# A hybrid attention layer on one core: the first attention's values and probabilities as scaled fp16 halves, two heads' values on chip, and the second attention's buffers laid out anew

## The chip, the cores and the metric

The kernel runs on one core of one Trainium2 chip. The metric is the device time of one execution in microseconds; the kernel before takes 2904.12 us (median of 3 runs, 2902.68 to 2909.47). PE is the matrix engine, with its weight loads shown apart as PEld; DVE, ACT and POOL are the vector, scalar and general engines; SP issues the DMAs.

## The reference, cut to what matters

One layer on a sequence of 1024 positions with 1024 channels: a feed-forward block, two attentions side by side on one normalised input, a gated merge of both, a second feed-forward block. The change touches the two attentions, above all the first:

```python
def diff_attention(q, k, v, cos, sin, lam_params, head_gain, lam_init):
    # q, k: 8 heads x 2 maps x 64;  v: 8 heads x 128;  T = 1024, causal
    q = apply_rope(q, cos, sin)
    k = apply_rope(k, cos, sin)
    lam = exp(sum(lp[0] * lp[1])) - exp(sum(lp[2] * lp[3])) + lam_init
    def block(i):                                  # 128 queries
        s = einsum('bqhcd,bkhcd->bhcqk', qb, k) * scale
        p = softmax(where(kpos <= qpos, s, NEG_INF))
        a = p[:, :, 0] - lam * p[:, :, 1]          # difference of the two maps
        return einsum('bhqk,bkhe->bqhe', a, v)
    o = rmsnorm(o, head_gain) * (1.0 - lam_init)
```

The second attention (16 heads of 64, two groups that share keys and values) adds a compressed, a selected and a window branch, each with its own softmax. With 16 blocks of which 16 are selected, the selected branch is causal attention over all blocks.

## The kernel before

**Precision.** Products that need more than one pass are made of two parts: a value is split into a high part (`hi`, a copy by ACT to a shorter type) and a rest (`lo`, a subtraction by DVE). `split` (L89, L85) makes fp32r parts; `split16` and the second attention make fp16 parts. `mm3` (L52 to L54) adds the three products hi·hi, hi·lo and lo·hi. Transposes, scores and projections work on 4-byte operands.

**Order of the work.** A first feed-forward block; `prelim`, which projects keys, values and queries for the second attention, its compressed branch, and the first two heads' values of the first attention; `da_phase`, the first attention; `ns_phase`, the second attention; `proj`, the merge; a second feed-forward block. The instructions are emitted in program order with priorities; a planner puts each engine's queue in order by priority and by its own model of time. `K.tc.high_priority(offset=-n)` sets a stretch of code n places back. Tiles come from pools opened on a stack; a pool that closes gives its space to later ones, and a tile on that space waits for the last use of the tile that lay there.

**Values of the first attention.** `v_da_unit(K, h)` projects the values of a head in two halves of 512 positions (`tb`). The product goes to a bank `gm`, is scaled by DVE to `vt` (L650), transposed by four matmuls (L653) into another tile of `gm`, split by ACT and DVE into `vh` and `vl`, and both are stored to DRAM (`s_v`, L658). `da_load_parts` loads a head's keys (L1031) and both parts of its values (L1038) at the start of the head; the pool of values holds one head (two tiles).

**The first attention.** `da_phase` goes through eight heads in four steps `m` of 256 queries. `da_queries` loads queries; `da_scores` makes two maps of scores in a pair of banks (L909), finds the maximum with DVE (L916), exponentiates with ACT into tiles `Pt` (L918), and combines the maps with POOL and DVE (L948 to L952). One step later `finish` calls `da_pv`: `tr_split` transposes up to four blocks into a bank `tr` (L964) and splits them to `th` and `tl`; three matmuls for each pair of blocks add to `o` (L991 to L993). After every second step `da_finish` copies `o` to `ob`, and one step later `da_finish2` normalises it with a chain over PE (L1008), ACT, POOL and DVE (L1014) and stores `yo` (L1018).

**The filler.** Between scores, `Filler` emits parts of independent products at a low priority: the units of `da_units` for heads 4 to 7 (queries, keys, values), then 16 gate units and 8 of the projection `pda_unit`, which reads the stored result of the first attention. `fill.pace(units, steps)` spreads them over the steps. In the filler there is one `gm` bank.

**The second attention.** `ns_phase` opens its pools on the space of the first attention's, loads queries, values and masks, and goes through 16 heads with the same scheme: `ns_scores` writes probabilities to a tile `P0` and a window tile `P1` from a ring of six pairs (two in one pool, four in another), `ns_pv` adds to `o` with fp16 operands (L1146, L1147).

Of the kernel before, what the change touches and what calls it, by code (L numbers as in the profile page):

```python
# [7 lines left out]
F32 = mybir.dt.float32  # L8
# [10 lines left out]
P = 128  # L19
# [623 lines left out]
def v_da_unit(K, h):  # L643
    nc = K.nc
    w = load_w(K, K.A["win"][C_VDA + h])
    for tb in range(NTB):
        ps = K.gm.tile([P, TB], F32, tag="gm", name="gm")
        yield from fill_gemm(K, ps, w, K.h[tb])
        vt = K.mp.tile([P, TB], F32, tag="m13", name="vt")
        nc.vector.tensor_tensor(out=vt, in0=ps, in1=K.R[tb], op=ALU.mult)  # L650
        tr = K.gm.tile([P, 4, P], F32, tag="gm", name="tr")
        for j in range(4):
            nc.tensor.transpose(tr[:, j], vt[:, j * P:(j + 1) * P], K.ident)  # L653
        vh = K.mp.tile([P, 4, P], F32R, tag="rh", name="vh")
        vl = K.mp.tile([P, 4, P], F32R, tag="rl", name="vl")
        split(nc, vh, vl, tr)
        for hl, t in ((0, vh), (1, vl)):
            nc.sync.dma_start(out=K.s_v[h][hl][:, tb * 4:tb * 4 + 4], in_=t.bitcast(F32))  # L658
# [300 lines left out]
def tr_split(K, blocks):  # L959
# [5 lines left out]
    dt = F16 if K.narrow else F32R  # L965
    hi = K.tp.tile([P, TB], dt, tag="th", name="th")
    lo = K.tp.tile([P, TB], dt, tag="tl", name="tl")
    if K.narrow:
        nc.scalar.activation(out=hi[:, 0:n], in_=tr[:, 0:n], func=AF.Copy)  # L969
        nc.vector.tensor_tensor(out=lo[:, 0:n], in0=tr[:, 0:n], in1=hi[:, 0:n], op=ALU.subtract)  # L970
    else:
        split(nc, hi[:, 0:n], lo[:, 0:n], tr[:, 0:n])
# [48 lines left out]
def da_load(K, h):  # L1021
    drain([da_load_parts(K, h)])


def da_load_parts(K, h):
    nc = K.nc
    p, s0 = h // 2, (h % 2) * 2
    K.k = []
    for c in range(2):
        t = K.kp.tile([P, T], F32R, tag="k", name="kt")  # L1030
        nc.sync.dma_start(out=t.bitcast(F32), in_=K.s_k[p][:, :, s0 + c].rearrange("h a d t -> (h a) d t"))  # L1031
        K.k.append(t)
        yield
    K.v = []
    K.vv[h] = K.v
    for hl in range(2):
        t = K.vp.tile([P, 8, P], F32R, tag="v", name="vt")
        nc.sync.dma_start(out=t.bitcast(F32), in_=K.s_v[h][hl])  # L1038
        K.v.append(t)
        yield  # L1040
# [676 lines left out]
```

## Time and profile before

| what | value |
|---|---|
| median of 3 runs | 2904.12 us (2902.68 to 2909.47) |
| the profiled execution | 2903.55 us, span 2901.8 us |
| mean granted clock of PE | 0.988 |
| PE busy | 2791.5 us, 96% of the span |
| DVE, ACT, POOL busy | 1995.2, 1370.8, 789.2 us |
| DMA | 476.12 MB, mean 164 GB/s |

The span runs from the first to the last instruction. PE's busy time counts overlapping matmuls once, and the ends of matmuls are modelled, so the rate of PE is better read from one start to the next. The first attention lies at about 975 to 1472 us, the second at 1472 to 2065. Line numbers are those of the kernel before.

### The profile page before, as it was taken

To read this page: it belongs to the slowest core of one execution; us is meant where nothing else is said; L and a number is where in the kernel's file an instruction comes from. 1 tells how busy PE (TensorE), PEld (TensorE's weight loads), DVE (VectorE), ACT (ScalarE), POOL (GpSimd) and SP (SyncE) were. 2 spreads that over 40 slices of the span, in tenths; PEclk is the share of its full clock that TensorE was granted. 3 is DMA by queue.
4 is the path that set the end of the run, shared out by engine and by line. 5 is a ranking of instruction groups with operands and counts; after the bars stand their busy time and mean duration, and the time that the engine had idled before them with its cause. 6 is when DMAs were issued, how large, how long until landed. Compare 5 with 4: busy or idle time off the path is not lost. (4 is left out here: it accounts for less than half of the span.)

```text
span 2901.8 us, 40199 instructions
## 1 busy us (share of the span) xinstructions
PE 2791.5 (96%) x14278; PEld 2055.0 (71%) x14278; DVE 1995.2 (69%) x3356; ACT 1370.8 (47%) x2351; POOL 789.2 (27%) x701
## 2 busy tenths in 40 slices
PE   8999999999999899989989999999999999999998
PEld 6644447887788778868877778888787844444886
DVE  7866865666688467667777777777333977676566
ACT  7533424442333245445566666677433653333443
POOL 3134321000045212322233333333242414223001
PEclk9999999999999999999999999999999999999999
DMA  4355547655446645444432226222843246445854
GB/s 164 121 202 179 177 170 269 217 189 148 153 174 211 221 155 177 167 162 160 155 122 89 88 80 201 88 88 81 315 149 120 80 146 221 163 171 172 293 182 144
DMA packets 212137, 476.12 MB, mean 164 GB/s; under 512 B 20832, under 2 KB 39520, under 8 KB 211936
## 3 DMA queue, kind: packets, MB, share of 16 engines
q1 hardware_dynamic: 211936, 473.55, 48.1%
q8 instruction: 112, 1.84, 0.3%
q14 instruction: 89, 0.73, 0.1%
HBM read 312.52 MB, written 160.96 MB: 163 GB/s over the span
## 5 line engine op out<-in xcount | busy, mean ns | idle before, releaser
L405 PEld LDWEIGHTS <-w 128*128 128x128 f16 x3024 | 297.3, 99 | 381.8 <-issue 32.2
L52 PE MATMUL gm<-hi,whi 128*128 128x512 f32 x880 | 351.0, 399 | 6.0 <-ACT whi L89 3.3
L54 PE MATMUL gm<-hi,wlo 128*128 128x512 f32 x880 | 348.7, 397 | 0.5 <-DVE wlo L85 0.5
L53 PE MATMUL gm<-lo,whi 128*128 128x512 f32 x880 | 348.0, 395 | 0.0
L405 PE MATMUL Y<-tf,w 128*128 128x512 f16 x1296 | 297.5, 384 | 16.7 <-DVE u L443 13.9
L909 PE MATMUL S<-kt,qt 128*128 128x320 f32 (+5 forms) x1152 | 270.1, 352 | 27.2 <-ACT Pt L918 12.4
L85 DVE TENSOR_TENSOR wlo<-st,whi 128x1024 fp32r<-128x1024 f32 x154 | 197.6, 1301 | 114.2 <-ACT whi L89 113.2
L916 DVE CUSTOM_DVE_ANT_0 S<-S,slab 128x896 f32<-128x896 f32 (+7 forms) x320 | 224.3, 710 | 56.1 <-PE S L909 50.3
L53 PE MATMUL acc<-wlo,whi 128*128 128x512 f32 (+1 forms) x628 | 244.4, 389 | 1.0 <-DVE wlo L85 1.0
L89 ACT ACTIVATE whi<-st 128x1024 fp32r<-128x1024 f32 x154 | 160.7, 1057 | 178.8 <-PE acc L54 106.4
L54 PE MATMUL acc<-whi,wlo 128*128 128x512 f32 (+1 forms) x628 | 243.0, 390 | 0.0
L52 PE MATMUL acc<-whi 128*128 128x512 f32 (+1 forms) x628 | 240.7, 387 | 0.4 <-DVE xd L590 0.4
L970 DVE TENSOR_TENSOR tl<-tr,th 128x512 f16<-128x512 f32 (+2 forms) x304 | 183.9, 616 | 45.9 <-ACT th L969 44.9
L909 PEld LDWEIGHTS S<-kt,qt 128*128 128x128 f32 x1152 | 182.7, 190 | 43.9 <-ACT Pt L918 14.6
L1098 POOL TENSOR_SCALAR Ps<-Ps,l 128x384 f32<-128x384 f32 (+7 forms) x128 | 102.0, 797 | 372.6 <-DVE l L1096 246.0
L969 ACT ACTIVATE th<-tr 128x512 f16<-128x512 f32 (+2 forms) x304 | 159.2, 539 | 79.0 <-PE tr L964 62.6
L405 PE MATMUL X<-h,w 128*128 128x512 f16 x864 | 195.3, 379 | 0.6 <-ACT s L415 0.5
L52 PEld LDWEIGHTS gm<-hi,whi 128*128 128x128 f32 x880 | 168.1, 191 | 39.0 <-ACT whi L89 3.5
L54 PEld LDWEIGHTS gm<-hi,wlo 128*128 128x128 f32 x880 | 167.8, 191 | 36.3 <-DVE wlo L85 1.4
L53 PEld LDWEIGHTS gm<-lo,whi 128*128 128x128 f32 x880 | 167.7, 191 | 30.8
L85 DVE TENSOR_TENSOR wlo<-wst,whi 128x1024 fp32r<-128x1024 f32 x103 | 137.9, 1340 | 45.6 <-ACT whi L89 36.8
L521 POOL TENSOR_TENSOR u<-u,u 128x512 f32<-128x512 f32 x36 | 52.8, 1467 | 345.0 <-DVE sa L102 163.2
(330 smaller groups left out, 6167.9 us busy)
## 6 DMA issues: line engine op xcount, KB each, us to landing
wst<-in_win_dram SPq DMA_DIRECT2D x55, 512.0 KB
sw<-w2s SPq DMA_DIRECT2D x44, 512.0 KB
st<-sw SPq DMA_DIRECT2D x88, 256.0 KB
st<-saT SPq DMA_DIRECT2D x88, 256.0 KB
a<-in_f1w_dram SPq DMA_DIRECT2D x36, 512.0 KB
a<-in_f2w_dram SPq DMA_DIRECT2D x36, 512.0 KB
st<-saB SPq DMA_DIRECT2D x66, 256.0 KB
qt<-sq SPq DMA_DIRECT2D x128, 128.0 KB
```

Source lines behind the costliest of these rows:

```text
L52: first = nc.tensor.matmul(out, lhsT=w[0][:, wk], rhs=x[0], start=start, stop=False, skip_group_check=skip)
L53: nc.tensor.matmul(out, lhsT=w[0][:, wk], rhs=x[1], start=False, stop=False, skip_group_check=skip)
L54: nc.tensor.matmul(out, lhsT=w[1][:, wk], rhs=x[0], start=False, stop=stop, skip_group_check=skip)
L85: return nc.vector.tensor_tensor(out=lo, in0=src, in1=hi.bitcast(F32), op=ALU.subtract)
L89: nc.scalar.activation(out=hi, in_=src, func=AF.Copy)
L405: K.mark = nc.tensor.matmul(o, lhsT=w[:, a, m * h + k], rhs=x[k][:, b], start=start and k == 0 and i == 0, stop=k == h - 1 and i == 2, ski ...
L521: nc.gpsimd.tensor_tensor(out=a, in0=a, in1=b, op=ALU.mult)
L909: K.last = nc.tensor.matmul(S[:, o:o + n], lhsT=q, rhs=k[:, k0 + c:k0 + c + n], start=i == 0, stop=i == 1)
L916: nc.vector.tensor_tensor_reduce(out=sv, in0=sv, in1=mv, scale=-0.125, scalar=BIG, op0=ALU.add, op1=ALU.min, accum_out=nm)
L969: nc.scalar.activation(out=hi[:, 0:n], in_=tr[:, 0:n], func=AF.Copy)
L970: nc.vector.tensor_tensor(out=lo[:, 0:n], in0=tr[:, 0:n], in1=hi[:, 0:n], op=ALU.subtract)
L1098: nc.gpsimd.tensor_scalar(out=p[:, 0:n], in0=p[:, 0:n], scalar1=l[:, c:c + 1], scalar2=P_NS, op0=ALU.mult, op1=ALU.mult)
```

## The change

Scores stay as they were. The values are stored once, as fp32; per head, the sum of their squares gives a power of two (`pow2_scale`) by which they are scaled when they are split into fp16 halves on chip. `lam` takes a scale of its own, so that the difference of the maps fits fp16; the inverse of both scales (`dsi`) rides on the copy of `o` to `ob`. The value unit handles two heads and puts the transposes of each half behind the first part of the next product; in the filler they use the `tr` banks instead of `gm`. The value pool holds two heads' halves (four fp16 tiles) and one loaded tile. Values are loaded ahead: at step 2 of the head before (heads 1, 2, 3, 5, 7) or at the start of their own head (4, 6), and split at step 3 of the head before or behind the scores of step 0. `th`/`tl` have three pairs instead of two. The second attention's pools are split up and opened in another order with padding, and the last `da_finish2` gets priority offset -250 instead of -100.

```diff
-def v_da_unit(K, h):
...
+def v_da_unit(K, heads):
+    late = None
+    for h in heads:
+        w = load_w(K, K.A["win"][C_VDA + h])
+        for tb in range(NTB):
+            ps = K.gm.tile([P, TB], F32, tag="gm", name="gm")
+            for k, _ in enumerate(fill_gemm(K, ps, w, K.h[tb])):
+                if k == 0 and late:
+                    v_da_store(K, *late)
+                yield
+            vt = K.mp.tile([P, 2, TB], F32, tag=("m13", "m42")[tb], name="vt")
+            K.nc.vector.tensor_tensor(out=vt[:, 0], in0=ps, in1=K.R[tb], op=ALU.mult)
+            late = h, tb, vt
+    v_da_store(K, *late)
+
+def v_da_store(K, h, tb, vt):
+    nc = K.nc
+    pool, tag = (K.gm, "gm") if K.fill is None else (K.tr, "tr")
+    tr = pool.tile([P, TB], F32, tag=tag, name="tr")
+    for j in range(4):
+        nc.tensor.transpose(tr[:, j * P:(j + 1) * P], vt[:, 0, j * P:(j + 1) * P], K.ident)
+    vr = K.mp.tile([P, 2, TB], F32, tag=("rh", "rl")[tb], name="vr")
+    nc.scalar.activation(out=vr[:, 0], in_=tr, func=AF.Copy)
+    nc.sync.dma_start(out=K.s_v[h][:, tb * 4:tb * 4 + 4], in_=vr[:, 0].rearrange("p (j d) -> p j d", j=4))
+    nc.scalar.activation(out=vt[:, 1], in_=vt[:, 0], func=AF.Square, accum_out=K.dss[:, 2 * h + tb:2 * h + tb + 1])
...
@@ tr_split
-    dt = F16 if K.narrow else F32R
...
+    hi = K.tp.tile([P, TB], F16, tag="th", name="th")
+    lo = K.tp.tile([P, TB], F16, tag="tl", name="tl")
+    nc.scalar.activation(out=hi[:, 0:n], in_=tr[:, 0:n], func=AF.Copy)
+    nc.vector.tensor_tensor(out=lo[:, 0:n], in0=tr[:, 0:n], in1=hi[:, 0:n], op=ALU.subtract)
@@ da_finish
-    nc.scalar.activation(out=ob, in_=o, func=AF.Copy)
+    nc.scalar.activation(out=ob, in_=o, func=AF.Copy, scale=K.dsi[:, h:h + 1])
...
+def da_load_values(K, h):
+    K.vr = K.vrp.tile([P, 8, P], F32, tag="vr", name="vr")
+    K.nc.sync.dma_start(out=K.vr, in_=K.s_v[h])
+
+def da_split_values(K, h, pool, tag):
+    nc = K.nc
+    tot = pool.tile([P, TB], F32, tag=tag, name="tot")[:, 0:1]
+    for tb in range(NTB):
+        nc.tensor.matmul(tot, lhsT=K.ones, rhs=K.dss[:, 2 * h + tb:2 * h + tb + 1], start=tb == 0, stop=tb == 1)
+    s, v = pow2_scale(K, K.cst, tot, 51, K.pinv)
+    nc.vector.tensor_copy(out=K.dsi[:, h:h + 1], in_=v)
+    t = [K.vp.tile([P, 8, P], F16, tag="v", name="vt") for _ in range(2)]
+    nc.scalar.activation(out=t[0], in_=K.vr, func=AF.Copy, scale=s)
+    nc.vector.scalar_tensor_tensor(out=t[1], in0=K.vr, scalar=s, in1=t[0], op0=ALU.mult, op1=ALU.subtract)
+    K.vv[h] = t
...
@@ prelim
+        s, v = pow2_scale(K, K.cst, l2, 51)
+        nc.vector.tensor_scalar(out=K.lam, in0=K.lam, scalar1=s, scalar2=None, op0=ALU.mult)
+        nc.vector.tensor_copy(out=K.pinv, in_=v)
...
-B_DV = 2
+B_DV = 4
...
-B_DT = 2
+B_DT = 3
+PAD = (1152, 1536)
...
@@ da_phase
+                if h in (4, 6):
+                    da_load_values(K, h)
                 for m in range(4):
                     qt = q0 if h + m == 0 else da_queries(K, h, m)
...
+                    if m == 2 and h + 1 in (1, 2, 3, 5, 7):
+                        da_load_values(K, h + 1)
                     res = da_scores(K, h, m, qt, fill.step)
                     if pend:
                         finish(*pend)
+                    if m == 0 and h in (4, 6):
+                        da_split_values(K, h, K.tr, "tr")
+                    if m == 3 and h + 1 in (1, 2, 3, 5, 7):
+                        da_split_values(K, h + 1, K.tr, "tr")
                     pend = (h, m, res)
...
-        with K.tc.high_priority(offset=-100):
+        with K.tc.high_priority(offset=-250):
             da_finish2(K, *K.fin)
...
@@ ns_phase
-        K.pp, K.n_p = [open_pool(K, ctx, "npa", 2), open_pool(K, ctx, "npb", B_NP - 2)], 0
...
+        pad("pad0", PAD[0])
+        K.nvp = {(0, 0): pool("nv00"), (0, 1): pool("nv01")}
+        K.pcp.append(pool("npc1"))
+        K.pp = [None] * B_NP
+        third = pool("pw2")
+        pad("pad1", PAD[1])
+        K.tp = pool("nt", B_NT)
+        K.pp[5] = [pool("ps5")]
+        for i in range(3):
+            K.pp[i] = [pool(f"ps{i}")]
+        K.pp[2].append(third)
+        K.pp[0].append(pool("pw0"))
+        pad("pad2", PAD[1])
+        K.nvp[1, 0] = pool("nv10")
+        K.op = pool("no")
+        K.pp[1].append(pool("pw1"))
+        K.pp[3] = [pool("ps3"), pool("pw3")]
+        K.pp[4] = [pool("ps4"), pool("pw4")]
+        K.pp[5].append(pool("pw5"))
```

## Rows read from the trace of the kernel before

**Rows 1.** Busy time of each engine in four stretches of the two attentions (first attention's start, first attention, the change to the second, second attention). Columns: stretch, its length, then busy us and instructions of PE, PEld, DVE, ACT and POOL, then the granted clock, the share of the DMA engines and GB/s.

```profile
975.00:1041.00 66.00, 55.60 (x244) 45.09 (x244) 32.37 (x65) 17.86 (x35) 11.47 (x11) 0.95 0.55 184
1041.00:1472.00 431.00, 404.47 (x2159) 342.85 (x2158) 309.77 (x638) 218.63 (x449) 122.15 (x121) 0.98 0.47 162
1472.00:1500.00 28.00, 20.17 (x113) 15.98 (x113) 14.05 (x50) 13.86 (x38) 10.37 (x18) 0.88 0.38 127
1500.00:2065.00 565.00, 551.76 (x3758) 452.76 (x3757) 429.47 (x1097) 377.81 (x857) 178.07 (x242) 1.00 0.35 116
```

**Rows 2.** Timeline of PE in the first attention: the first of nine value matmuls of 256 columns that follow one another, the first of the three of 128 columns behind them, and the instruction behind those. Columns: start us, us, engine, line, operation, tiles, shape, count.

```profile
1261.07 0.28 PE L991 MATMUL o<-th,vt 128*128 128x256 f32 x1
...
1262.14 0.22 PE L991 MATMUL o<-th,vt 128*128 128x128 f32 x1
...
1262.42 0.45 PE L909 MATMUL S<-kt,qt 128*128 128x256 f32 x2
```

**Rows 3.** The same view in the second attention, whose values and probabilities are fp16: two matmuls of 128 columns with the instruction behind them, and the first of four of 256 columns with the instruction behind those.

```profile
1703.24 0.22 PE L1146 MATMUL o<-th,vt 128*128 128x128 f16 x1
...
1703.36 0.39 PE L964 MATMUL tr<-ident,Pw 128*128 128x128 f32 x2
...
1703.58 0.27 PE L1146 MATMUL o<-th,vt 128*128 128x256 f16 x1
...
1704.02 0.49 PE L964 MATMUL tr<-ident,Ps 128*128 128x128 f32 x3
```

**Rows 4.** The instructions that read a value tile, by line: count, then shortest, median and longest duration in ns, first and last start, shapes.

```profile
L991 PEld LDWEIGHTS o<-th,vt x160: 186/188/337, 1049.3 to 1471.6; 128*128 128x128 f32 x160
...
L991 PE MATMUL o<-th,vt x160: 218/281/579, 1049.5 to 1471.7; 128*128 128x256 f32 x128, 128*128 128x128 f32 x32
...
L1146 PEld LDWEIGHTS <-vt x608: 94/98/149, 1485.8 to 2062.0; 128*128 128x128 f16 x152
```

**Rows 5.** Timeline of PE: the long waits of the first attention and the start of the second. In brackets the idle time before the row and what ended it.

```profile
980.13 0.69 PE L909 MATMUL S<-kt,qt 128*128 128x128 f32 x2 [4.08 <-DMA kt<-sk]
...
1014.25 0.66 PE L653 MATMUL tr<-ident,vt 128*128 128x128 f32 x4 [2.68 <-DVE vt L650]
...
1023.85 0.66 PE L653 MATMUL tr<-ident,vt 128*128 128x128 f32 x4 [2.14 <-DVE vt L650]
...
1195.25 0.58 PE L991 MATMUL o<-th,vt 128*128 128x256 f32 x1 [3.33 <-ACT th L89]
...
1272.72 1.22 PE L909 MATMUL S<-kt,qt 128*128 128x512 f32 x2 [6.09 <-ACT Pt L918]
...
1291.16 0.55 PE L991 MATMUL o<-th,vt 128*128 128x256 f32 x1 [2.73 <-DMA vt<-sv]
...
1483.98 1.22 PE L909 MATMUL S<-kt,qt 128*128 128x512 f32 x2 [7.37 <-ACT Ps L918]
```

**Rows 6.** Busy time in stretches of 5 us behind those waits (columns as in rows 1; the granted clock is the number before the DMA share).

```profile
1020.00:1025.00 5.00, 2.75 (x13) 1.74 (x12) 3.27 (x10) 2.38 (x5) 0.58 (x1) 1.00 0.35 127
...
1195.00:1200.00 5.00, 4.75 (x12) 3.80 (x13) 4.39 (x10) 2.96 (x8) 0.69 (x2) 0.50 0.27 104
...
1270.00:1275.00 5.00, 2.28 (x8) 2.09 (x9) 2.79 (x8) 2.32 (x6) 0.00 (x0) 0.50 0.27 99
...
1290.00:1295.00 5.00, 3.84 (x10) 3.11 (x11) 4.03 (x8) 2.29 (x5) 2.69 (x2) 0.50 0.77 248
...
1480.00:1485.00 5.00, 1.02 (x3) 0.84 (x4) 1.77 (x4) 2.27 (x7) 1.83 (x2) 0.55 0.28 105
```

**Rows 7.** Timelines of the DMA issues on SP, of ACT and of DVE: the instructions at which three of those waits began.

```profile
1258.57 0.42 SPq L658 DMA_DIRECT2D sv<-vh  x1
...
1271.51 0.60 ACT L89 ACTIVATE vh<-tr 128x512 fp32r<-128x512 f32 x1 [6.04 <-DMA sv<-vh]
...
1282.71 1.73 SPq L1038 DMA_DIRECT2D vt<-sv  x2
...
1481.95 0.75 DVE L1014 SCALAR_TENSOR_TENSOR ob<-ob,hgain,yr 128x512 f32<-128x512 f32 x1 [3.42 <-POOL yr L160]
...
1482.73 0.63 ACT L89 ACTIVATE yo<-ob 128x512 fp32r<-128x512 f32 x1 [4.27 <-DVE ob L1014]
...
1483.27 0.56 ACT L918 ACTIVATE Ps<-S,nm 128x384 f32<-128x384 f32 x1
```

**Rows 8.** Instructions of the kinds that the change adds or removes, by line over the whole execution: count, then shortest, median and longest ns, first and last start, shapes.

```profile
L683 PE MATMUL tot<-vone,ones x2: 251/262/272, 731.0 to 731.2; 128*128 128x1 f32 x2
...
L323 ACT ACTIVATE w<-a,sc x90: 1132/1134/1152, 92.2 to 2637.8; 128x1024 f16<-128x1024 f32 x90
...
L324 DVE SCALAR_TENSOR_TENSOR w<-a,sc,w x90: 1268/1280/2291, 99.3 to 2644.2; 128x1024 f16<-128x1024 f32 x90
...
L104 DVE TENSOR_SCALAR sa<-sa x20: 141/153/163, 35.1 to 2627.9; 128x1 int32<-128x1 int32 x19, 128x4 int32<-128x4 int32 x1
...
L674 ACT ACTIVATE vj<-tr x4: 597/597/598, 712.1 to 729.9; 128x512 bf16<-128x512 f32 x4
...
L85 DVE TENSOR_TENSOR vl<-tr,vh x16: 673/691/692, 771.8 to 1288.3; 128x512 fp32r<-128x512 f32 x16
```

**Rows 9.** Groups of instructions with their shapes, the first from the first attention, the second from the second. Columns: line, engine, operation, tiles, shapes, count, busy us, mean ns, idle before and what ended it.

```profile
L85 DVE TENSOR_TENSOR tl<-tr,th 128x512 fp32r<-128x512 f32 x48 | 32.9, 685 | 6.1 <-ACT th L89 6.1
...
L970 DVE TENSOR_TENSOR tl<-tr,th 128x512 f16<-128x512 f32 x176 | 119.7, 686 | 27.9 <-ACT th L969 27.3
```

More of the change, by code (lines that the diff above doesn't have):

```diff
@@ L640, in rope_pair @@
             cmp(tb, uh, ul)
-def v_da_unit(K, h):
-    nc = K.nc
[L645 to L658, printed above, removed]
+def v_da_unit(K, heads):
[13 more added lines that the diff above has]
+def v_da_store(K, h, tb, vt):
+    nc = K.nc
+    pool, tag = (K.gm, "gm") if K.fill is None else (K.tr, "tr")
[6 more added lines that the diff above has]
+    nc.scalar.activation(out=vt[:, 1], in_=vt[:, 0], func=AF.Square, accum_out=K.dss[:, 2 * h + tb:2 * h + tb + 1])
 def v_ns_unit(K, br):
@@ L1030, in da_load_parts @@
         t = K.kp.tile([P, T], F32R, tag="k", name="kt")
-        nc.sync.dma_start(out=t.bitcast(F32), in_=K.s_k[p][:, :, s0 + c].rearrange("h a d t -> (h a) d t"))
+        K.nc.sync.dma_start(out=t.bitcast(F32), in_=K.s_k[p][:, :, s0 + c].rearrange("h a d t -> (h a) d t"))
         K.k.append(t)
         yield
[L1034 to L1040, printed above, removed]
+def da_load_values(K, h):
[12 more added lines that the diff above has]
+    K.vv[h] = t
 def ns_load_key(K, i):
@@ L1055, in ns_load_values @@
         for br in range(2):
-            pool, tag = (K.mp, "m42") if g and br else (K.kp, f"v{g}{br}")
-            t = pool.tile([P, 8, P], F16, tag=tag, name="vt")
+            pool = K.mp if g and br else K.nvp[g, br]
+            t = pool.tile([P, 8, P], F16, tag="m42", name="vt")
             K.nc.sync.dma_start(out=t, in_=K.s_v2[br][g])
@@ L1087, in ns_scores @@
         qs = [t[:, (i % 4) * P:(i % 4 + 1) * P] for t in qt]
[L1088 removed]
+        pools = K.pp[K.n_p % B_NP]
         K.n_p += 1
[L1090 to L1091 removed]
+        p0 = pools[0].tile([P, T], F32, tag="P0", name="Ps")
+        p1 = pools[1].tile([P, 5 * P], F32, tag="P1", name="Pw")
         scores(K, [(q, K.nk[g, 0], 0) for q in qs], w, K.slab[:, T - w:T], nm[:, 0:1], p0, l[:, 0:1])
@@ L1261, in mix @@
         K.lam = cst.tile([P, 2], F32, name="lam")
+        K.dss = cst.tile([P, 16], F32, name="dss")
+        K.dsi = cst.tile([P, 8], F32, name="dsi")
+        K.pinv = cst.tile([P, 1], F32, name="pinv")
         K.hgain = cst.tile([P, 8], F32, name="hgain")
@@ L1309, in prelim @@
         nc.vector.tensor_scalar(out=K.lam[:, 1:2], in0=K.lam[:, 1:2], scalar1=-LAM_INIT, scalar2=None, op0=ALU.add)
+        l2 = c0.tile([P, 1], F32, name="l2")
+        nc.vector.tensor_tensor(out=l2, in0=K.lam[:, 1:2], in1=K.lam[:, 1:2], op=ALU.mult)
+        nc.vector.tensor_scalar(out=l2, in0=l2, scalar1=1.0, scalar2=None, op0=ALU.add)
+        s, v = pow2_scale(K, K.cst, l2, 51)
+        nc.vector.tensor_scalar(out=K.lam, in0=K.lam, scalar1=s, scalar2=None, op0=ALU.mult)
+        nc.vector.tensor_copy(out=K.pinv, in_=v)
         K.kbh = c0.tile([P, 2, 2, 4, NC], F32R, name="kbh")
@@ L1374, in da_phase @@
             if n == 2:
-                early = da_load_parts(K, 0)
-            if n >= 2:
-                next(early)
-            if n == 5:
+                da_load(K, 0)
+            if n == 3:
+                da_load_values(K, 0)
+            if n == 4:
                 q0 = da_queries(K, 0, 0)
+                da_split_values(K, 0, K.gm, "gm")
             drain([f()])
@@ L1553, in body @@
         K.s_kv = dr.tile([2, 2, 4, 32, T], F32, name="skv")
-        K.s_v = [[dr.tile([P, 8, P], F32, name=f"sv{h}_{i}") for i in range(2)] for h in range(8)]
+        K.s_v = [dr.tile([P, 8, P], F32, name=f"sv{h}") for h in range(8)]
         K.s_v2 = [[dr.tile([P, 8, P], F16, name=f"sv2{h}_{i}") for i in range(2)] for h in range(2)]
```

46 lines of the change are left out of this document (19 added, 27 removed).

## The prediction, written before the change was timed

> **What bounds the kernel now.** I read the busy time by stretches first, then the timeline of PE in the stretches that the diff touches, then the queues of the engines at each long wait. PE bounds both attentions, but not equally. In the second attention PE is busy 551.76 of 565 us at clock 1.00; in the first it is 404.47 of 431 at 0.98, in the 66 us that lead into it 55.60 at 0.95, and in the 28 us between the attentions 20.17 at 0.88 [rows 1]. So a shorter PE instruction is worth its time nearly everywhere, and a wait of another engine is worth something only if it ends as a wait of PE. Seven such waits are in the view [rows 5]: for keys (4.08), for a value tile ahead of its transposes (2.68 and 2.14), for `th` (3.33), for a probability buffer (6.09), for the stored values (2.73), and at the start of the second attention (7.37). Behind the longer ones the clock is halved: 0.50 in the stretches from 1195, 1270 and 1290 us, 0.55 from 1480; behind the wait of 2.14 us it stays at 1.00 [rows 6]. The work that a halved stretch holds costs half its busy time again.
>
> **The sum, part by part.** It is made against the profiled execution: 2903.55 us around a span of 2901.8, which is 0.6 us under the median of 2904.12. No term is finer than that.
>
> *fp16 halves in the value matmuls.* The count stays at three for each pair of blocks. Nine with 256 columns take 1.07 us from the first to what follows, 119 ns each; three with 128 take 0.28, 93 ns [rows 2]. In the second attention, where both operands are fp16, four with 256 take 0.44 us, 110 ns, and two with 128 take 0.12, 60 ns [rows 3]. There are 3 x 128 of the wide and 3 x 32 of the narrow form [rows 4]: 384 x 9 ns + 96 x 33 ns = 6.7 us less. Below, it is nothing, if each group waits for `tl` anyway; I take 6.7, since these rows are the same operation.
>
> The weight load alone falls from 188 to 98 ns [rows 4]. [...]
>
> *`tr_split` in the first attention.* The same two instructions with fp16 outputs: the subtraction takes 685 ns with fp32r and 686 with fp16 [rows 9], so nothing. The halved tiles allow three pairs of `th`/`tl`, not two; a gain of up to 2 us is possible and I take none.
>
> *Transposes of the values put off.* They now follow the first three matmuls of the next product, and the last ones their own product. The waits of 2.68 and 2.14 us stood in front of just these transposes [rows 5]. Three matmuls of 512 columns, an estimated 0.7 us at the 119 ns for 256 [rows 2], would cover that much of each, so 1.4 is the lower bound and 4.8 the upper; other ready matmuls can go in between too, and I take 3. Inside the filler the transposes move from the only `gm` bank to the `tr` banks, which `tr_split` shares; each of eight such stores holds one until ACT has copied it, 0.6 us [rows 8]. Between 0 and 8 x 0.6 = 4.8 us; I take +2.
>
> *One store of the values.* The subtraction `vl` goes (16 x 0.69 us of DVE [rows 8]), half the stores and half the bytes go from SP's queue, and the two halves of a head use different tiles. That takes away the wait of 6.09 us: the copy `vh` stood on ACT 6.04 us for the store of the previous `vh`, which SP had issued 13 us before, and the exponentials behind it on ACT were what PE waited for [rows 5, 7]. With it goes half of the 2.28 us of work that ran behind it at half clock [rows 6]: 6.1 + 1.1 = 7.2. In its place the next use of the tile `rh` is a product later; if that still isn't late enough the term is 0.
>
> *Values of two heads on chip.* The value load of head 4 was issued at 1282.71, when the last value matmul of head 3 gave the buffers free, and PE waited for it until 1291.16 [rows 5, 7]: 8.4 us for two tiles, about 4.2 for the one tile of the new load. Heads 1, 2, 3, 5 and 7 now load two steps ahead; 4 and 6 at the head's start, a step ahead of the first use. A step is about 431/32 = 13 us [rows 1], against 4.2 plus the split; SP's issue order (keys, values, queries) stands between, so the margin is not sure. I take the wait and half the 3.84 us behind it [rows 5, 6]: 2.7 + 1.9 = 4.6 less; at worst 0.
>
> *The split of the values per head, new.* On PE two matmuls with one column, each shown as two instructions of 0.26 us that start 0.1 to 0.2 us apart [rows 8]: 8 x 4 = 32 of them, 3.2 to 8.3 us; I take 4. On DVE six operations of 0.153 us, a copy like them and one of 1.28: 2.35 a head, 18.8 in all against 11.0 removed. On ACT 1.13 a head and 16 squares of 0.6: 18.6 us [rows 8]. I cost these two at nothing: DVE is busy 309.77 and ACT 218.63 of 431 us [rows 1]. If DVE's cover were gone, the 7.8 us would be the price; what can go wrong on ACT is the third rival. The scaling of `lam` is some nine small DVE operations, 1.4 us beside products of the preliminary part; the scale on `ob` rides on an instruction that was there.
>
> *The second attention's buffers and the last `da_finish2`.* PE's 7.37 us at the change of phases: all score banks were full, the exponentials stood behind `yo` on ACT, that waited 4.27 us for `ob` on DVE, and that 3.42 for POOL [rows 5, 7]. The lower priority puts this chain behind more of the second attention's work, and the new layout lays each early tile on one that is free by then. Its two stores are read only by `pda_load`, whose units stand behind eight gate units, so that lateness costs nothing unless the filler gets there first. At most 7.4 us and the clock's share of 20.17 x 0.12 = 2.4, so 9.8; at least 0, if the chain only stalls later; I take 7.
>
> *A stall of the new order.* PE's order is made anew, and the waits for keys (4.08) and for `th` (3.33, with half of 4.75 us behind it: 5.7) are not addressed [rows 5, 6]. One more of the latter kind at even odds: +2.9. Above, it is 5.7.
>
> Gains 6.7 + 3 + 7.2 + 4.6 + 7 = 28.5, costs 2 + 4 + 2.9 = 8.9: 19.6 us less, 2884.0 us. With all bounds at their best, the two unaddressed waits gone too, it would be some 42 us less, 2862.
>
> **The rivals.**
>
> *The second attention starts as late as before.* The chain is the last of its phase, and tiles of the second attention still lie on its buffers; moved back, `yo` may block the next exponentials in the same way. For it: ACT and DVE take their work in order [rows 7]. Against: the later it stands, the more scores are through. Then 7 us are missing: 2891.
>
> *The waits move.* Four of the five gains are single waits in one order of instructions, and a new order has its own. For it: the four waits have four different causes [rows 7]. If half of the 21.8 us returns elsewhere, 10.9 are missing: 2895, on the edge of what a measurement of this kernel can tell from no change (0.3%, 8.7 us).
>
> *The split blocks ACT.* This one ends on the other side. The fp16 copy waits on ACT for the loaded values and for the scale; behind it in the queue stand the exponentials, DVE waits for their sums and PE for the score banks. That is what `vh` did to PE once [rows 7], at 7.2 us. Seven heads are split inside the attention: from the third that stalls so the gain is lost (3 x 7.2 = 21.6 against 19.6), with four it is 2913, with all seven 2934. Against: the load precedes by a step or more and the scale needs nothing late. [...]
>
> *The change does not reach PE.* The value matmuls gain nothing behind `tl`, and waits return in full: 2900 to 2908.
>
> **How the numbers follow.** Forecast 0.45, with a range of its own of 2872 to 2891; better than it, down to 2862, 0.05; late start 0.17; moved waits 0.18, half of it beyond the edge; no effect 0.06; blocked ACT 0.09. Faster by over 0.3% is 0.45 + 0.05 + 0.17 + 0.09 = 0.76, within it 0.09 + 0.06 = 0.15, slower 0.09. The range reaches from 2866, which leaves out most of the best case, to 2899, which leaves out no effect and blocked ACT: 2 in 10 outside. The predicted time is the likeliest, 2884.
>
> **What would show it.** Right: value matmuls at some 110 and 60 ns from start to start; no wait on PE for a value tile, for stored values, or for a probability buffer held up by a store; PE busier than 94% in the first attention and a clock above 0.95 at the change of phases; preliminary part and both feed-forward blocks as they were. Wrong: ACT waiting at the fp16 copy of the values with exponentials behind it; PE waiting on a `tr` bank; a wait of 7 us at the first scores of the second attention; or a stall of several us at a place that the diff doesn't touch.

## The result, and the profile after

The changed kernel is slower: 2934.27 us (median of 4 runs, 2933.23 to 2941.68) against 2904.15 for the kernel before on the same chip, a ratio of 1.0108 with an interval of 1.0090 to 1.0126. The profiled execution has a span of 2931.4 us against 2901.8. The forecast was 2884, and nothing above 2899 was in its range.

The first view is the one of [rows 1], busy time of each engine in four stretches, now of the changed kernel; the stretches are set to the same places of the work (first scores, first value matmul, last output of the first attention, 28 us behind it, end of the second attention).

```profile
977.00:1041.00 64.00, 56.82 (x250) 46.50 (x251) 24.98 (x51) 18.19 (x35) 7.50 (x7) 0.93 0.55 177
1041.00:1505.00 464.00, 407.19 (x2187) 325.39 (x2186) 326.66 (x700) 233.78 (x480) 122.45 (x124) 0.94 0.40 138
1505.00:1533.00 28.00, 25.60 (x157) 21.12 (x156) 20.46 (x64) 19.05 (x47) 12.32 (x19) 1.00 0.42 151
1533.00:2092.00 559.00, 545.23 (x3713) 446.87 (x3712) 422.64 (x1083) 372.87 (x847) 177.44 (x238) 1.00 0.34 115
```

The first attention takes 464 us instead of 431 and PE is hardly busier in it (407.19 against 404.47 us), at clock 0.94 instead of 0.98: the loss is waiting. PE is busy 88% of this stretch, where the prediction's sign of being right asked for over 94%. The change of phases is better, as foretold: PE is busy 25.60 of 28 us at clock 1.00, not 20.17 at 0.88. The value matmuls now start some 110 and 60 ns apart (256 and 128 columns, medians in the timeline of PE), as foretold too.

The next view is the timeline of PE, its long waits in the first attention, as in [rows 5] (brackets: idle time before the row, and what ended it).

```profile
982.12 0.66 PE L919 MATMUL S<-kt,qt 128*128 128x128 f32 x2 [3.57 <-DMA kt<-sk]
...
1155.12 0.37 PE L997 MATMUL o<-th,vt 128*128 128x256 f16 x1 [8.05 <-ACT th L977]
...
1284.61 0.79 PE L919 MATMUL S<-kt,qt 128*128 128x256 f32 x2 [10.58 <-ACT Pt L928]
...
1347.59 0.79 PE L919 MATMUL S<-kt,qt 128*128 128x512 f32 x1 [10.27 <-ACT Pt L928]
...
1403.66 0.80 PE L919 MATMUL S<-kt,qt 128*128 128x512 f32 x1 [8.09 <-ACT Pt L928]
...
1488.88 1.22 PE L1014 MATMUL tot<-sq,ones 128*128 128x512 f32 x1 [4.76 <-ACT sq L1007]
```

The wait for keys is there as before (3.57, before 4.08). The waits for the stored values (2.73) and at the second attention's first scores (7.37) [rows 5] are not in it, nor the one of 6.09 us in its old form. In their place stand four of 8 to 11 us, all for ScalarE (ACT), and one of 4.76 at the last normalization but one. What ScalarE stood for is in its own timeline, with SP's DMA issues (SPq) beside it:

```profile
1138.77 1.71 SPq L1216 DMA_DIRECT2D wst<-in_win_dram  x1
...
1153.01 1.06 ACT L1226 ACTIVATE whi<-wst 128x1024 fp32r<-128x1024 f32 x1 [14.67 <-DMA wst<-in_win_dram]
...
1154.50 0.58 ACT L977 ACTIVATE th<-tr 128x512 f16<-128x512 f32 x1
...
1283.15 1.06 ACT L1226 ACTIVATE whi<-wst 128x1024 fp32r<-128x1024 f32 x1 [11.54 <-DMA wst<-in_win_dram]
1284.11 0.35 ACT L928 ACTIVATE Pt<-S,nm 128x128 f32<-128x128 f32 x1
...
1324.74 3.39 SPq L1036 DMA_DIRECT2D kt<-sk  x2
...
1330.51 3.08 SPq L1024 DMA_DIRECT2D syd<-yo  x2
...
1333.37 0.60 ACT L977 ACTIVATE th<-tr 128x512 f16<-128x512 f32 x1 [1.58 <-PE tr L974]
1345.68 0.63 ACT L155 ACTIVATE yr<-m 128x512 f32<-128x512 f32 x1 [11.71 <-DMA syd<-yo]
...
1346.88 0.56 ACT L928 ACTIVATE Pt<-S,nm 128x384 f32<-128x384 f32 x1
...
1397.53 0.63 ACT L155 ACTIVATE yr<-m 128x512 f32<-128x512 f32 x1 [5.84 <-DMA syd<-yo]
...
1402.42 0.63 ACT L157 ACTIVATE zr<-yr 128x512 f32<-128x512 f32 x1 [3.60 <-DMA syd<-yo]
```

Ahead of two of PE's waits ScalarE stands 11 to 15 us at the split of a filler weight (`whi`) whose load has not landed; counted from the filler's first load, the one that the split at 1153.01 needs was issued at 1138.77. Ahead of the other two it stands at the Newton iteration of the next normalization (`yr`, `zr`), whose tiles still hold outputs `yo` that are being stored. Right behind the instruction come `th` or an exponential, and PE waits for that. The values' split (L1054) never stood so in this kernel.

For the comparison of all kernels I cut each profiled execution at three places: the first scores (here 977.04), the last but one output `ob` of the first attention (1487.48; it lies ahead of the disturbance at the change of phases), and the first `pj` matmul, which ends the second attention (2088.97). The stretch between the last two cuts is called the seam below, since what differs in it lies near its start. Worked out from these rows, in us, the difference to the kernel before in brackets:

| kernel | to first scores | first attention | its end and second attention | rest | span |
|---|---|---|---|---|---|
| before | 975.2 | 482.7 | 604.3 | 839.6 | 2901.8 |
| after | 977.0 (+1.9) | 510.4 (+27.8) | 601.5 (-2.8) | 842.4 (+2.8) | 2931.4 |
| e1_free | 978.8 | 493.8 (+11.1) | 601.6 (-2.7) | 844.7 | 2918.8 |
| e2_yo | 978.8 | 501.3 (+18.6) | 601.2 (-3.1) | 842.0 | 2923.3 |
| e3_both | 976.0 | 484.2 (+1.5) | 601.2 (-3.1) | 843.9 | 2905.3 |
| e5_yo15 | 977.3 | 483.1 (+0.4) | 601.5 (-2.9) | 842.5 | 2904.4 |
| e8_notlate | 975.0 | 494.0 (+11.3) | 601.6 (-2.7) | 840.8 | 2911.4 |
| e11_noscale | 976.1 | 474.5 (-8.2) | 599.8 (-4.5) | 839.3 | 2889.7 |
| e13_oldlayout | 977.6 | 471.3 (-11.4) | 607.8 (+3.4) | 836.7 | 2893.4 |
| e4_before_late | 972.9 | 497.6 (+15.0) | 608.6 (+4.3) | 838.0 | 2917.1 |
| e6_layout | 972.7 | 483.1 (+0.5) | 604.8 (+0.5) | 839.2 | 2899.8 |
| e7_half | 974.4 | 471.4 (-11.2) | 609.6 (+5.3) | 841.1 | 2896.5 |
| e9_onestore | 973.9 | 475.8 (-6.9) | 608.2 (+3.9) | 839.1 | 2897.0 |
| e10_late | 973.1 | 498.7 (+16.0) | 607.1 (+2.7) | 838.8 | 2917.7 |
| e12_late_yo | 975.3 | 480.9 (-1.8) | 608.4 (+4.1) | 840.7 | 2905.3 |
| e14_half_layout | 973.0 | 475.4 (-7.3) | 615.5 (+11.1) | 840.4 | 2904.2 |

The rest, which no kernel touches, varies by 8 us (836.7 to 844.7), which is how far a single execution can be off; the timed ratios below decide, the table says where. One difference lies ahead of the first scores: the changed kernel and the seven made from it (e1 to e3, e5, e8, e11, e13) reach them at 975.0 to 978.8 us, the kernel before and the seven made from that at 972.7 to 975.3. In the first eight PE stands 3.3 to 5.2 us just ahead of them, in the others it does not; the profile names nothing that it waits for, and no run looked into it.

### The profile page after: what moved, and what is told of

It reads as the page before. It is cut to its first block, busy times and chain, and to the rows that moved or that the text cites. A ratio compares the mean times of both kernels' runs of the same rounds, so it can differ in the third digit from the quotient of the medians.

```text
span 2931.4 us, 40289 instructions
## 1 busy us (share of the span) xinstructions
PE 2792.2 (95%) x14310; PEld 2037.6 (70%) x14310; DVE 2003.4 (68%) x3414; ACT 1389.2 (47%) x2391; POOL 787.4 (27%) x701
## 5 line engine op out<-in xcount | busy, mean ns | idle before, releaser
L978 DVE TENSOR_TENSOR tl<-tr,th 128x512 f16<-128x512 f32 (+2 forms) x384 | 234.1, 618 | 69.2 <-ACT th L977 67.9
L977 ACT ACTIVATE th<-tr 128x512 f16<-128x512 f32 (+2 forms) x384 | 203.4, 542 | 136.4 <-PE tr L974 120.1
```

## The experiments

**Theory A, late weights.** The filler counts its work in parts, 16 to a weight. It splits weight n as soon as the table `free_at` says that weight n - 2 is done (plus `SLACK`), and each split lets a further load go. The change also merges the value weights of two heads into one entry of the list `cs` that this table is made from (`[C_VDA + 2 * p, C_VDA + 2 * p + 1]` in place of two entries). For a unit with two weights the table has 24 and 32 parts after the unit's start, which is right for a pair that is rotated. The two-head value unit has two weights too, but its first is done after 16. So the split of the next unit's first weight, and a load behind it, come 8 parts late, and ScalarE meets a load that is still under way. **Theory B, the outputs' store.** `yo` lies on the same two buffers (tags `yr` and `zr`) that the next `da_finish2` writes; in the new order the store goes out late (behind the key loads on SP) and the next `da_finish2` comes early. **Rival C:** any new order has such waits, and taking one away only moves it.

**e1_free** corrects the table, **e2_yo** puts the outputs of heads 4 to 7 in tiles of the rotary pool, **e3_both** does both:

```
 e1: -  self.free_at.append(at + (16 if len(ws) == 1 else 24 + 8 * z))
     +  self.free_at.append(at + (16 * (z + 1) if isinstance(w, tuple) or len(ws) == 1 else 24 + 8 * z))
     (value weights are handed over as (W[c],))
 e2: -  yo = [K.op.tile([P, TB], F32R, tag=t, name="yo") for t in ("yr", "zr")]
     +  if h < 4: (as before)
     +  else:
     +      yt = K.mp.tile([P, 2, TB], F32R, tag=("rl", "m42")[H], name="yo")
     +      yo = [yt[:, i] for i in range(2)]
```

> The changed kernel; only the filler's table of when a weight slot is free is mended: a value unit of two heads now counts 16 parts for each weight (16, 32), not 24 and 32 as a pair of rope weights. Theory of the late weights: the split of the next unit's first weight, and with it the load of its second, goes 8 parts earlier, so ACT no longer stands 14.67 us (at 1153) and 11.54 us (at 1283) for a weight; PE's waits of 8.05 and 10.58 us go, with some 2 us of half clock behind each: 22 us less, 2912. Theory that waits only move in any new order: within 8 us of 2934. Theory that the stored results (syd) are the main cause: the waits at 1337 and 1395 stay as they are and the gain is that of the two weights alone.

> The changed kernel; only the split result yo of heads 4 to 7 gets space of its own (two tiles of the rope pool that lie idle there) and no longer lies on yr and zr of the next normalisation. Theory of the stored results: ACT no longer stands 11.71 and 5.84 + 3.60 us for the store of yo; PE's waits of 10.27 and 8.09 us go, with some 2 us of half clock behind each: 22 us less, 2912, while the two waits for weights stay. Theory that waits only move: within 8 us of 2934.

> Both edits, the filler's table and the space for yo. If the two causes are separate and complete: 44 us less than the changed kernel, 2890, about 14 below the kernel before. If waits only move: no better than the better of the two alone.

Measured: e1_free 2920.44 us, ratio to the kernel before 1.0061 (1.0045 to 1.0078); e2_yo 2923.75, 1.0072 (1.0056 to 1.0088); e3_both 2910.34, 1.0021 (1.0011 to 1.0032). Against the 1.0108 of the change that is 14, 10 and 25 us, where 22, 22 and 44 were expected: each is a cause, and they add up. e2_yo could not give all of it, since the outputs ahead of the wait of 10.27 us are head 3's, which it leaves on the old tags (10.18 us in its trace). e1_free takes away PE's waits of 8.05 and 10.58 us and gets 14 of these 18.6 us back. In it the same load as above is issued 14.5 us earlier, and the split that needs it waits for nothing:

```profile
1124.27 0.45 SPq L1216 DMA_DIRECT2D wst<-in_win_dram  x1
...
1141.09 1.04 ACT L1226 ACTIVATE whi<-wst 128x1024 fp32r<-128x1024 f32 x1
```

The waits of ScalarE from 975 to 1510 us, summed by cause (us in total, times, longest), in the changed kernel,

```profile
ACT whi L1226 <- DMA wst<-in_win_dram: 39.2, 4, 14.7
ACT yr L155 <- DMA syd<-yo: 17.6, 2, 11.7
ACT zr L157 <- DMA syd<-yo: 4.2, 2, 3.6
```

in e1_free,

```profile
ACT yr L155 <- DMA syd<-yo: 18.3, 2, 11.3
ACT whi L1226 <- DMA wst<-in_win_dram: 8.5, 3, 3.7
```

and in e2_yo:

```profile
ACT whi L1230 <- DMA wst<-in_win_dram: 37.9, 4, 14.1
ACT yr L155 <- DMA syd<-yo: 11.6, 1, 11.6
```

Each edit takes away its own kind and leaves the other, which rival C does not explain. One long wait is left in e3_both, that of head 3's second half, still on the old tags (PE and ACT of e3_both):

```profile
1327.72 1.22 PE L919 MATMUL S<-kt,qt 128*128 128x512 f32 x2 [11.11 <-ACT Pt L928]
...
1325.82 0.63 ACT L155 ACTIVATE yr<-m 128x512 f32<-128x512 f32 x1 [13.11 <-DMA syd<-yo]
```

**e5_yo15** moves that half too (`if 2 * h + H < 7:` in place of `if h < 4:`).

> The run with both undone (weights' slots freed on time, normalized outputs of heads 4 to 7 in tiles of the rotary pool), and the outputs of the second half of head 3 in such a tile too. The trace of e3_both kept one long wait: 11.11 us on TensorE ahead of scores at 1327.72, behind 13.11 us of ScalarE for the store of head 3's outputs. Theory B (the store on the tags of the next normalization): that wait goes and the time falls by 8 to 11 us from 2910.3, to 2899 to 2903. Rival C (waits only move): another wait of about the same length stands later, 2907 to 2912.

Measured: 2900.78 us, 0.9998 (0.9989 to 1.0006): by the ratios 7 us under e3_both, a little less than theory B had it, and 32 us under the change. With both causes out, the whole loss against the kernel before is gone; what is left is as fast as that. Its longest waits on PE are now of other kinds:

```profile
1277.65 0.60 PE L919 MATMUL S<-kt,qt 128*128 128x320 f32 x1 [3.88 <-DMA qt<-sq]
...
1331.63 0.61 PE L919 MATMUL S<-kt,qt 128*128 128x320 f32 x1 [4.36 <-ACT vt L1058]
...
1461.87 2.07 PE L1014 MATMUL tot<-sq,ones 128*128 128x512 f32 x2 [4.81 <-ACT sq L1007]
```

The second is put down to the split of the values (`vt`, L1058), but that is only the last of three instructions that ScalarE ran after it had stood 3.44 us for another late weight (ACT of e5_yo15):

```profile
1289.60 1.15 ACT L1058 ACTIVATE vt<-vr,sc 128x1024 f16<-128x1024 f32 x1 [4.75 <-DVE sc L106]
...
1328.99 1.06 ACT L1230 ACTIVATE whi<-wst 128x1024 fp32r<-128x1024 f32 x1 [3.44 <-DMA wst<-in_win_dram]
```

The first of these two lines is a wait of the values' split for its scale, as the prediction's third rival had it. e1_free (3.81 us), e3_both (4.40) and e8_notlate (4.88) have it too; PE worked on through it (5.00 of the 5 us from 1284 in e5_yo15).

**e4_before_late** puts theory A's error into the kernel before (first value weight of a pair: 24 for 16).

> The kernel before with only the late table of the changed one: the slot of the first value weight of a pair counts as free after 24 parts, not 16. Theory of the late weights: the next unit's second weight is loaded 8 parts later here too, so a wait of ACT for a weight of some 10 us appears behind each of the two value units, and the time grows by 10 to 22 us, to 2914 to 2926. Theory that waits only move: within 5 us of 2904.

Measured: 2920.91 us, 1.0063 (1.0048 to 1.0078), 17 us more. The time fits, the trace does not: ScalarE waits for weights only 5.4 us longer than in the kernel before (19.6 against 14.2), and the waits on PE are others:

```profile
ACT whi L1210 <- DMA wst<-in_win_dram: 19.6, 4, 8.1
...
1335.11 0.79 PE L52 MATMUL gm<-hi,whi 128*128 128x512 f32 x1 [4.32 <-DVE vt L744]
...
1471.86 2.07 PE L1008 MATMUL tot<-sq,ones 128*128 128x512 f32 x2 [4.69 <-ACT sq L1001]
```

So this run shows that the table is worth some 17 us, not by which wait; waits at other places are what rival C would have. Theory A rests on e1_free.

**The terms one by one.** **e7_half** is the kernel before with fp16 halves alone, **e6_layout** with the second attention's pools and the offset of -250 alone, both copied from the change.

```
 e7: -  dt = F16 if K.narrow else F32R          (tr_split: always F16)
     -  vh, vl = ... F32R ...; split(nc, vh, vl, tr)
     +  vh, vl = ... F16 ...; Copy on ScalarE, subtract on VectorE
     -  K.s_v, vt: F32, F32R
     +  K.s_v, vt: F16
 e6: the diff's part in ns_phase, ns_scores, ns_load_values, and offset=-250
```

> The kernel before with fp16 halves of values and probabilities in the first attention alone (no power-of-two scale is applied, which is left out of the computation; halves are stored and loaded as two fp16 arrays; order, loads and buffers as before). By the prediction's row the value matmuls give 6.7 us; by the busy time of e3_both (128.1 against 138.1 us for 480 matmuls) 10 us. The value arrays move half the bytes, which takes up to 4 us more off the waits for them. So 2890 to 2897. If TensorE is not what sets the first attention's pace, 2901 to 2906.

> The kernel before with the second attention's new buffers and the offset of -250 alone. The prediction's term: 7 us off, 2896 to 2898. The traces of after and e3_both: from the last half head of the first attention to the first value matmul of the second 5.3 us less than before, so 2898. Rival: the 7.37 us only become another wait at the same seam, 2902 to 2905.

Measured: e7_half 2895.44, 0.9978 (0.9969 to 0.9986), 6.4 us less; e6_layout 2900.44, 0.9999 (0.9990 to 1.0009), nothing. The halves give 11.2 us in the first attention (table), as the busy time of its 480 value matmuls falls from 138.1 to 127.2 us, and 5 are lost again behind it. The wait at the second attention's first scores stays, at the length that it had before (7.37), so it is not what lost them; in the 80 us behind the cut the mean clock is 0.89, before 0.96.

```profile
1475.89 1.22 PE L910 MATMUL S<-kt,qt 128*128 128x512 f32 x2 [7.38 <-ACT Ps L919]
```

In e6_layout that wait is down to 3.19 us, and the seam is no shorter: PE is busy 584.85 us in it, before 581.39, and the mean clock of its first 80 us is 0.94, before 0.96. Why is open.

```profile
1486.89 0.50 PE L909 MATMUL S<-kt,qt 128*128 128x256 f32 x2 [3.19 <-ACT Pw L918]
```

**e9_onestore** adds to e7_half one tile and one store for both halves, the tag alternating between `rh` and `rl`.

> As e7_half (2895.4), with both halves of a value half in one tile, whose tag alternates with the half of the sequence, and one store in place of two. The prediction's term: 7.2 us off, from the wait of ScalarE for the store of the halves; e7_half still has it (5.23 us of TensorE ahead of scores at 1265.12). So 2888 to 2891. Rival (the wait moves): 2894 to 2897.

Measured: 2898.74, 0.9982 (0.9973 to 0.9991): nothing. ScalarE's wait for the previous store of values, 4.9 us in e7_half, is gone, and PE has waits of that size and below at other places:

```profile
1275.40 0.90 PE L907 MATMUL S<-kt,qt 128*128 128x320 f32 x2 [4.33 <-DMA qt<-sq]
...
1283.75 0.28 PE L985 MATMUL o<-th,vt 128*128 128x256 f16 x1 [2.40 <-DMA vt<-sv]
```

**The transposes put off.** **e8_notlate** takes that part out of e5_yo15 (each value half is transposed and stored at once), **e10_late** puts it into e9_onestore, **e12_late_yo** gives e10_late the tiles of e5_yo15 for `yo`.

```
 e8:  -  if k == 0 and late: v_da_store(K, *late)
      +  v_da_store(K, h, tb, vt)       (behind the multiplication by R)
 e10: +  late = h, tb, vt kept in K.late from head to head; its store after the first part of the next product
 e12: +  the edit of e5_yo15 to yo
```

> As e5_yo15, with the transposes and the store of each value half made at once instead of after the next projection's first part. The prediction counted 3 us for putting them off: 3 us above e5_yo15. If the waits for the evicted tile (2.1 to 2.7 us each for about four of the eight in the first attention) all come back: 8 to 11 us above. If ScalarE and VectorE set the pace there: no difference.

> As e9_onestore, with the transposes and the split of each value half put off to after the first part of the next value projection, in a PSUM tile shared with the probabilities, the two heads' units still apart in the filler's table. By the prediction 3 us less than e9_onestore; by the difference of e8_notlate and e5_yo15 up to 14 us less. If that difference was the order of the two-head unit and not the transposes: within 2 us of e9_onestore.

> As e10_late (2919.5), with the normalized outputs from the second half of head 3 on in tiles of the rotary pool, as in e5_yo15. In the trace of e10_late ScalarE waits 22.5 us in all for the store of these outputs (yr 12.2, zr 10.3), and TensorE four times behind it (4.67, 1.87, 3.96 and 1.85 us, 12.4 in all). Theory B (the store on the tags of the next normalization is what the new order runs into, whatever put the order there): 10 to 14 us off, 2905 to 2909. If the put-off transposes cost by themselves: 2916 to 2921.

Measured: e8_notlate 2915.42, 1.0042 (1.0031 to 1.0054), 13 us above e5_yo15; e10_late 2919.46, 1.0064 (1.0050 to 1.0077), 24 us above e9_onestore; e12_late_yo 2902.98, 0.9997 (0.9989 to 1.0005). The first two seem to say opposite things of one edit, and both expectations missed. The traces show what stands there. In e8_notlate a weight is late again, with the mended table,

```profile
1087.92 0.37 PE L992 MATMUL o<-th,vt 128*128 128x256 f16 x1 [7.00 <-ACT th L972]
...
1086.33 1.06 ACT L1225 ACTIVATE whi<-wst 128x1024 fp32r<-128x1024 f32 x1 [16.14 <-DMA wst<-in_win_dram]
```

in e10_late it is the outputs' store (ScalarE, 975 to 1510 us),

```profile
ACT yr L155 <- DMA syd<-yo: 12.2, 2, 6.5
ACT zr L157 <- DMA syd<-yo: 10.3, 4, 3.6
```

of which e12_late_yo has one wait left, and it is 19 us faster:

```profile
ACT zr L157 <- DMA syd<-yo: 2.3, 1, 2.3
```

That is more than the 12.4 us of PE's waits behind the store in e10_late; half clock behind them is the likely rest (13.0 us of PE's work from 1329.0 to 1337.6 and 1383.8 to 1392.8, at 0.50 and 0.53, of which half, an estimated 6.5 us, is lost). It shows theory B in a kernel without two-head units and without the scale. What putting off is worth by itself these runs do not give: in e8_notlate its absence costs 13 us, and e12_late_yo, which has it, stands 4 us above e9_onestore, at the edge of their intervals. That the weights come late in e8_notlate although the table is right is a point for rival C.

**e11_noscale** is e5_yo15 without the sums, the squares and the power of two.

```
 e11: -  tot, pow2_scale, 2 matmuls a head; Square with accum_out
      -  activation(t[0], K.vr, Copy, scale=s); scalar_tensor_tensor(t[1], ...)
      +  activation(t[0], K.vr, Copy); tensor_tensor(t[1], K.vr - t[0])
```

> As e5_yo15 (2900.8), without the per-head scale: no squares and no sums of the values, no 32 matmuls for them, no power of two (the values are halved as they are, which leaves the scale out of the computation). The prediction counted 4 us on TensorE for the sums and the split of a head; the trace of e5_yo15 has 4.2 us for the 32 matmuls, and 4.36 us of waiting for one head's split at 1331.63. So 2893 to 2897. If the order of the rest sets the time: 2900 to 2903.

Measured: 2891.47, 0.9961 (0.9949 to 0.9974), the fastest of all and 11 us under e5_yo15. The first attention's stretch of [rows 1] is now shorter than in the kernel before (426 against 431 us), at the same clock:

```profile
1041.00:1467.00 426.00, 397.65 (x2132) 315.30 (x2131) 312.32 (x638) 224.55 (x456) 126.23 (x123) 0.98 0.43 148
```

**e13_oldlayout** puts the old pools and the old offset into e11_noscale, **e14_half_layout** the new ones into e7_half.

> As e11_noscale (2891.5), with the second attention's buffers and the last normalization's offset of -100 as they were before. By the prediction's term the layout is worth 7 us: 2898. If e6_layout holds here too (nothing): 2890 to 2893. If TensorE's 4.83 us ahead of the last normalization's sum, which e11_noscale has at 1452.04 and the kernel before has not, come from the offset: 2887 to 2889.

> The kernel before with two parts of the change alone: fp16 halves in the first attention (as e7_half, 2895.4) and the second attention's buffers with the offset of -250 (as e6_layout, 2900.4). From the last output of the first attention to the next stage the profiled executions with the new buffers take 583.3 to 586.1 us, those with the old ones 589.9 to 591.3. If that gain adds to the halves': 2888 to 2891. If, as in e6_layout, the first attention's new order takes it back: 2894 to 2897.

Measured: e13_oldlayout 2894.70, 0.9965 (0.9952 to 0.9978), not to be told from e11_noscale; e14_half_layout 2904.99, 1.0004 (0.9995 to 1.0013), 8 us above e7_half and above all that was expected. By the table the seam is 8.0 us longer with the old pools in e13_oldlayout, whose wait of 7.43 us is that of [rows 5] again,

```profile
1477.58 0.80 PE L918 MATMUL S<-kt,qt 128*128 128x512 f32 x1 [7.43 <-ACT Ps L927]
```

and 5.9 us longer than in e7_half with the new pools in e14_half_layout, where the chain of [rows 7] (DVE `ob`, ACT `yo`, exponential) stands as before:

```profile
1484.52 0.69 PE L910 MATMUL S<-kt,qt 128*128 128x128 f32 x2 [7.77 <-ACT Pw L919]
...
1482.45 0.63 ACT L89 ACTIVATE yo<-ob 128x512 fp32r<-128x512 f32 x1 [4.27 <-DVE ob L1011]
```

The new pools are laid against the first attention's buffers of the change; on other ones they may meet tiles that come free later; that is argued, not shown, since addresses were not moved one by one. The wait of 4.76 us ahead of the last normalization but one, 1.17 us in the kernel before, is none of the pools' or the offset's: e13_oldlayout has it too (4.83), with both as they were.

## Why the prediction was wrong, step by step

**The step that failed** is the new order's stall. The prediction gave "a stall of the new order" 2.9 us, at most 5.7, and had no term at all for what brings it: the merged entry in `cs`, which makes the filler's table wrong for value units, and `yo`, which the change does not touch but whose time between store and next use it shortens. (The prediction's own last sign of being wrong, a stall at a place that the diff doesn't touch, fits the second of the two.) Measured, they are 14 us (e1_free) and 10 + 7 us (e2_yo; e5_yo15 against e3_both, by their ratios), together the 32 us between the change and e5_yo15 within a microsecond. The margin at the second place is in the kernel before: the store of head 3's second half, issued at 1304.16, has 13.8 us until `yr` is written again (SP and ACT of the kernel before),

```profile
1304.16 4.98 SPq L1018 DMA_DIRECT2D syd<-yo  x2
...
1317.96 0.62 ACT L155 ACTIVATE yr<-m 128x512 f32<-128x512 f32 x1
```

and in the change 3.5 us pass from the issue of the same store at 1330.51 to the end of the last work ahead of `yr` (1333.37 + 0.60), after which ScalarE stands until 1345.68. A short margin alone is no wait, though: a later store of the kernel before, issued at 1457.07, has 4.2 us until `yr` is written at 1461.27, and nothing waits. The one that stalls stands behind two key loads on SP.

**The rivals.** "The split blocks ACT" had the mechanism (ScalarE stands at one instruction, the exponentials behind it are late) and a range whose upper end the time met (2913 to 2934), but the wrong instruction: in the changed kernel the fp16 copy of the values waits for nothing, the weights' split and the Newton iteration do. That the size fits is luck. "The waits move" let half of the removed waits return and stopped at 2895; it needed no bound from what was removed. In the trace of the changed kernel ScalarE runs nothing within the waits of 14.67 and 11.71 us, and `th` and an exponential start 1.49 and 1.20 us behind their ends.

**fp16 halves, -6.7.** Right by the time: -6.4 (4.1 to 9.0 by the interval) in e7_half. That the two agree so closely is partly luck: in the first attention it is more, 11 us, and 5 are lost at the seam, which the term did not have. By line over the whole execution the value matmuls of e7_half keep this median (count, shortest/median/longest ns):

```profile
L988 PE MATMUL o<-th,vt x160: 218/273/421, 1048.2 to 1463.7; 128*128 128x256 f16 x128, 128*128 128x128 f16 x32
```

against 281 ns in [rows 4].

**One store, -7.2.** Did not hold: the wait went and others of 2 to 4 us came, 0 in time (e9_onestore). **Transposes put off, -3 and +2.** Not settled: 13 us for them in one kernel (e8_notlate), 4 against them in another (e12_late_yo), both with the order of the rest changed. **Values of two heads on chip, -4.6.** The wait for the stored values went; waits for queries (3.88) and behind a late weight (4.36) took its place in e5_yo15. It was not tried alone. Together the three give about nothing: the first attention of e13_oldlayout, which has all of them and the halves without scale, is as long as that of e7_half, 471.3 and 471.4 us.

**The split of the values per head, +4.** Too small: the scale alone, which is what e11_noscale takes out, is 11 us against e5_yo15; the split itself stays in that run. The 32 matmuls take 4.2 us, as costed. The other 7 came with the work on ScalarE and VectorE, which was costed at nothing, or with the new order: without the scale, the split's wait for it and PE's wait of 4.36 us are both gone. Which of the two it was is open.

**The second attention's buffers, -7.** In the changed kernel the wait of 7.37 us went, as foretold, and the seam gained 2.8 us; 3.6 came back in the wait of 4.76 ahead of the last normalization but one. Against the old pools with the same source for the first attention (e13_oldlayout) it is 8.0, so the mechanism held there. On the first attention of the kernel before it did not: the seam was no shorter in e6_layout and 5.9 us longer in e14_half_layout. In time the part is worth nothing that was measured (e6_layout, e13_oldlayout), and beside the halves alone it costs 8 us.

**So the sum** without the two causes: halves -6.4 and scale +11 make +4.6 us, and e5_yo15 measured -0.6 (interval -3.2 to +1.7). If the parts add, the other four are then worth some 5 us together, of which the table shows 2.9 at the seam. That they add is not shown: e14_half_layout is 8 us above the sum of e7_half and e6_layout.

## What to carry to other kernels

Where one unit of work is merged or split, every table that says when its inputs and buffers come free is part of the change, and is to be costed like an instruction. Ahead of a new order, list the transfers that an instruction waits for with others queued behind it and the time each has from issue to use, and what stands ahead of each in the DMA queue; one with little to spare can be a wait of 8 to 11 us in the next order, and its price is not bounded by the waits that the change removes. A gain measured at one place is not a gain in time until the order around it has been seen to stay.

## What the hardware showed that I had not expected

While ScalarE and PE of the changed kernel both waited for a weight or a store, the DMA engines were 26, 43, 26 and 30% busy (shares from 1147.1 to 1153, 1274.1 to 1283.1, 1337.4 to 1345.6 and 1398.9 to 1402.4 us), and in the 5 us from 1155, 1285, 1348 and 1403, right behind that, 9 to 27% (busy time in stretches of 5 us, the second within a wait, the others behind one; the last three columns are granted clock, DMA share, GB/s):

```profile
1285.00:1290.00 5.00, 5.00 (x15) 3.76 (x15) 3.04 (x10) 1.96 (x7) 3.85 (x5) 0.54 0.26 100
...
1340.00:1345.00 5.00, 0.00 (x0) 0.00 (x0) 0.00 (x0) 0.00 (x0) 0.00 (x0) 0.58 0.26 102
...
1403.00:1408.00 5.00, 4.34 (x11) 3.14 (x12) 3.84 (x9) 2.82 (x9) 3.76 (x4) 0.50 0.10 32
```

In the middle stretch every engine stands still, at 102 GB/s. SP had issued two key loads from 1324.74, a weight's load, the outputs' two stores from 1330.51 and query loads behind them; ScalarE went on 15.2 us after the first store's issue. Why no more of them was busy was not tried.

Behind the four long waits PE's clock is at about one half (0.51 in the 5 us from 1155, 0.54 and 0.50 in those from 1285 and 1403, 0.50 from 1347.6 to 1350), and matmuls of 512 columns that follow one another start 0.43 us apart (from 1285.62), against 0.23 us at clock 1.00 (from 1292.75): a wait costs more than its length. What taking one out gives is another matter: 12.4 us of waits came back as 19 us in e12_late_yo against e10_late, but 18.6 as 14 in e1_free and 11.1 as 7 in e5_yo15 against e3_both, where other waits came. In [rows 6] the clock was at half (0.50) already behind waits of 3.33 and 2.73 us (the latter with one of 1.30 us just ahead of it).
